# A line through HBM in place of a spreading product for four norms, with moved edges and block order

## The chip, the cores and the metric

The kernel runs on one core of one Trainium2 chip. The core has TensorE (PE in the profile; PEld is its weight load), VectorE (DVE), ScalarE (ACT), GpSimd (POOL) and SyncE (SP, which here mostly issues DMA transfers). SBUF is the on-chip memory with 128 partitions, PSUM the memory into which TensorE accumulates. The metric is the device time of the program in microseconds, as the median of several runs. Times inside the program are from one profiled execution, counted from the start of its span.

## The reference

A two-layer decoder trunk over 512 tokens of width 1024, in float32. Cut to its steps:

```python
def rmsnorm(x, g):
    return x * lax.rsqrt(jnp.mean(x * x, axis=-1, keepdims=True) + EPS) * g

h = x
# layer 0
h = h + mixer_a(rmsnorm(h, norm_mix[0]))     # gelu(xn @ w_in) -> u, v; u * (W_s norm(v) + b) @ w_out
h = h + conv_ffn(rmsnorm(h, norm_ffn[0]))    # width-3 causal conv between up (1024 -> 2 x 2816) and silu(g)*u, then down
h = h + (p[0] @ w_pin) * sigmoid(rmsnorm(h, norm_ple[0]) @ w_gate + b_gate)
k, v = shared_kv(h, norm_kv, w_kv)
# layer 1
h = h + mixer_b(rmsnorm(h, norm_mix[1]), k, v)   # 16 query heads on 4 KV heads, window of 128, ALiBi, sinks
h = h + conv_ffn(rmsnorm(h, norm_ffn[1]))
h = h + (p[1] @ w_pin) * sigmoid(rmsnorm(h, norm_ple[1]) @ w_gate + b_gate)
return rmsnorm(h, norm_final)
```

Each rmsnorm needs one root per token. The norms are called n0 (norm_mix 0), nf0 (norm_ffn 0), np0 (norm_ple 0), n1 (norm_mix 1 and the shared K/V's gain), nf1 and np1 in the kernel.

## The kernel before, in words

**Layout.** The residual `h` lies transposed: eight tiles of 128 features x 512 tokens. A product of a weight and an activation is made of three float32r products (`mm3`, L190 to L192): high part times high, high times low, low times high. Each is one matmul of 128x128 weights on 512 columns. `mm3t` (L201 to L203) does the same with tokens on the output's partitions.

**Weights.** They arrive on SyncE's queue in pieces (`load`, L136) into a few raw buffers, and are cut in units of up to 1024 columns (`pump`): ScalarE casts the high part `wh` (L163) and VectorE subtracts to get the low part `wl` (L164). There are four unit buffers. `chunk` takes the next units and pumps up to `ahead` units further. The order in which a program line calls `pump` and `chunk` is the order in which casts and differences stand on ScalarE and VectorE; a raw buffer is free for the next load when its last difference has been made.

**Norms.** The gain is multiplied into the activations when they are split, and the root is applied after the product, since it is the same for all features of a token. `Norm.take` splits a tile and adds up its square; `turn` transposes the sum and reduces it (`quarter`, L313). `begin` makes a small product `ms` (L322) with the matrix `alike`, a scale and offset on VectorE (L364) and the power -1/2 on GpSimd (L366), giving `r`: the roots of 512 tokens as 8 columns, token 64*c + p on partition p, twice. Then it casts `r` to a high and a low half (`hl`). `rstd` (L353 to L356) calls `spread`: VectorE multiplies `hl` with a picked identity into `d` (128x512, L346), TensorE multiplies `d` with a matrix of ones (L350), so that every partition holds the whole line of 512 roots, and ScalarE copies it from PSUM to SBUF (L355). The readers multiply a product in PSUM by that line: `uz` (L594) for n0, `hs` (L403) for nf0 and nf1, `z` (L479) for np0. In `ffn` and `ple` `begin` is called after the first product of the block and `rstd` after the second; the readers come right after it. In n0 `begin` is called within the v products and `rstd` before the u products.

**Attention.** Sixteen steps work on score blocks. The dictionary `beside` (L763) gives what TensorE does between the steps: the products of the output projection w_o (`merge`), whose weights come in four chunks c = 0 to 3, and `more`, which pumps one unit ahead. `behind` adds an ordering edge between two instructions of one engine.

**The end.** The last per-layer embedding is computed with tokens on partitions. Block i (128 tokens) is computed in stretches n of 512 or fewer columns: `gate_t` makes its product `gt`, `gated_t` (L999) the sigmoid (`st`), the product with `pet` (L1016), the sum `hm` (L1032), its squares and the gain (L1044, L1048); `scaled` takes the root, `leaves` scales and sends the block. Block 3 has the stretches (3,0), (3,1), (3,2) and is sent by `end` in three pieces.

At the start of the program eight `idle` products (L240) run on TensorE before the first real one.

Of the kernel before, what the change touches and what calls it, by code (L numbers as in the profile page):

```python
# [8 lines left out]
F32 = mybir.dt.float32  # L9
F32R = mybir.dt.float32r  # L10
AF = mybir.ActivationFunctionType
# [32 lines left out]
FIRST = [(0, 0, 1), (1, 0, 1), (0, 1, 2), (1, 1, 2), (0, 2, 4), (0, 4, 8), (1, 2, 4), (1, 4, 8)]  # L44
IDLE = 8


@with_exitstack
def tile_yoco(ctx: ExitStack, tc: tile.TileContext, t, out: bass.AP, out_b: bass.AP):
# [7 lines left out]
    mp = ctx.enter_context(tc.tile_pool(name="mp", bufs=1))  # L57
    tp = ctx.enter_context(tc.tile_pool(name="tp", bufs=2))
    mmp = ctx.enter_context(tc.tile_pool(name="mmp", bufs=8, space=bass.MemoryType.PSUM))

# [218 lines left out]
    class Norm:  # L279


        def __init__(self, name, gains):
            self.name = name
            self.xs = [(xtiles(pool, f"{name}{i}", tags), g) for i, (pool, tags, g) in enumerate(gains)]
            self.acc = self.quarter = self.behind = None

# [28 lines left out]

        def begin(self, rows=1):


            if self.quarter is None:
                self.turn()  # L320
            ps = psum(f"{self.name}ms")[:, : S // 32]
            nc.tensor.matmul(ps, alike.rearrange("p a b -> p (a b)"), self.quarter, start=True, stop=True)  # L322
            ms = ps.rearrange("p (c r) -> p r c", r=2)
            n = S // 64
            r = inv_root([(slice(32 * q, 32 * (q + 1)), ms[32 * q : 32 * (q + 1), q % 2, :]) for q in range(4)],
                         self.name, n=n)
            def by_rows():
                self.rt = const.tile([P, NC], F32, tag="rows", bufs=2, name=f"{self.name}rows")
                r2 = r.rearrange("p (c e) -> p e c", e=2)
                for e in range(2):  # L330
                    nc.vector.tensor_copy(self.rt[64 * e : 64 * (e + 1)], r2[64 * e : 64 * (e + 1), e])

            if rows == 1:
                by_rows()

            self.hl = const.tile([P, n], F32R, tag="hl", bufs=1, name=f"{self.name}hl")
            nc.vector.tensor_copy(self.hl, r)
            nc.vector.tensor_sub(self.hl[64:], r[64:], self.hl[64:].bitcast(F32))
            if rows == 2:
                by_rows()  # L340
            return self.rt if rows else None
# [10 lines left out]

        def rstd(self):  # L353
            r = tp.tile([P, S], F32, tag="rstd", name=f"{self.name}rstd")
            nc.scalar.copy(r, self.spread(0, S // 64))  # L355
            return r  # L356
# [30 lines left out]
    def ffn(l, norm, nxt):  # L387
# [4 lines left out]
        def up(j):  # L392
            parts = chunk(256, KD)
            pss, cs = [], []
            for s in range(2):
                ps = psum(f"up{j}_{s}")
                mm3(ps, parts, xs, s * P)
                pss.append(ps)
                if j == 0:
                    rstds.append(norm.rstd() if s else norm.begin(rows=0))  # L400
            for s, ps in enumerate(pss):
# [63 lines left out]
    def ple(l, norm, nxt, pe):  # L465
        xs = norm.xs[0][0]
        rstd, held = None, []
        for c in range(4):
            parts = chunk(256, KD)
            for j in range(2):  # L470
                ps = psum(f"gate{c}_{j}")
                mm3(ps, parts, xs, j * P)
                held.append((2 * c + j, ps))
                if c == 0:
                    rstd = norm.rstd() if j else norm.begin(rows=0)
                if c or j:
                    for m, ps in held:
                        z = tp.tile([P, S], F32, tag="hs", name=f"z{m}")
                        nc.vector.tensor_mul(z, ps, rstd)  # L479
                        sg = tp.tile([P, S], F32, tag="sg", name=f"gs{m}")  # L480
                        nc.scalar.activation(sg, z, AF.Sigmoid, bias=v("ple_b_gate", l * KD + m))
                        nc.vector.tensor_mul(sg, sg, pe[m])
                        nc.vector.tensor_add(h[m], h[m], sg)
                        nxt.take(m)
                    held = []
# [15 lines left out]
    for q, k0, k1 in FIRST:  # L501
# [28 lines left out]
        if (q, k0) == (1, 2):  # L530
            rt = n0.begin()
    vps[0][0] = zv[0][:, :S]
# [80 lines left out]

    dram = ctx.enter_context(tc.tile_pool(name="dram", bufs=1, space=bass.MemoryType.DRAM))
    lines = dram.tile([KD, 2, P], F32, name="lines")
# [49 lines left out]
    def queries(ps, g, j):  # L665
# [15 lines left out]
        nc.scalar.copy(hi.bitcast(F32R), qf)  # L681
        nc.vector.tensor_sub(qf.bitcast(F32R), qf, hi)
        for e, q in enumerate(res):
# [62 lines left out]
    def merge(m, k0, k1, leave=False):  # L746


        if m // 2 not in box:
            box[m // 2] = chunk(256, KD, ahead=2)  # L750
        first = k0 == 0 or box.get(f"left{m}", False)
        if first:
            box[f"o{m}"] = psum(f"o{m}_{k0}")
        mm3(box[f"o{m}"], box[m // 2][k0:k1], o2[k0:k1], m % 2 * P, first=first, last=leave or k1 == KD)
        box[f"k{m}"], box[f"left{m}"] = k1, leave
        if leave:
            nc.vector.tensor_add(h[m], h[m], box[f"o{m}"])

    def more():

        pump(state["unit"] + 1)

    beside = {  # L763
# [13 lines left out]
        12: [(merge, 1, 2, 4, True), (merge, 2, 2, 4)],  # L777
        13: [(merge, 3, 0, 4), (more,)],
        14: [(merge, 4, 0, 4)],
        15: [(merge, 5, 0, 4)],  # L780
        16: [(merge, 2, 4, 6), (merge, 3, 4, 6), (merge, 0, 4, 6), (merge, 1, 4, 6)],
# [14 lines left out]
    def scores(i):  # L796
# [8 lines left out]
        for b in range(2):  # L805
# [8 lines left out]
            for j in range(2):  # L814
                e = 2 * b + j
                hd = GQ * g + e
                nc.vector.tensor_tensor_reduce(out=pr[:, e, :P], in0=far if n else near, in1=sc[:, j, 0, :],
                                               scale=-slope(hd), scalar=nsink[:, hd : hd + 1],
                                               op0=ALU.add, op1=ALU.min, accum_out=neg[:, e : e + 1])
        sm = at.tile([P, GQ], F32, tag="sm", bufs=2, name=f"sm{i}")  # L820
        for e in range(GQ):
            nc.scalar.activation(pr[:, e, :], pr[:, e, :], AF.Exp, bias=neg[:, e : e + 1], scale=-1.0,
                                 accum_out=sm[:, e : e + 1])
        live[i] = (pr, sm)
# [37 lines left out]
    def mix(i):  # L862
# [15 lines left out]
        for e in range(2):  # L878
            nc.vector.tensor_add(o[sides[e]], a[:, e], low[:, e])
        cols = slice(n * P, (n + 1) * P)  # L880
# [120 lines left out]
    def gated_t(i, n, ps):  # L1001
# [4 lines left out]
        if end:  # L1006
            box["sg"] = nc.scalar.activation(sg, ps, AF.Sigmoid, scale=r)
        else:
# [34 lines left out]
        if i < LAST:  # L1043
            nc.gpsimd.tensor_mul(hm, hm, grow[:, c0 : c0 + w])  # L1044
        else:
# [12 lines left out]
    def leaves(i, root):  # L1058
# [3 lines left out]
        for n in range(2):  # L1062
# [7 lines left out]
            if i == 2:  # L1070
                behind(ins, box["sg"])
            if i == 0:
# [13 lines left out]
    def end():  # L1086
        y = yt[0]
        nc.gpsimd.tensor_tensor(rfin, total[:, 2:3], minus_half[:, :1], op=ALU.pow)
        for c0, c1 in ((0, 384), (384, 640), (640, D)):
            if c0:  # L1090
# [12 lines left out]
    bias_rows()  # L1103
    for i, n in ((2, 0), (3, 0), (2, 1)):
        gated_t(i, n, gate_t(i, n))
    root = scaled(2)
    for n in (1, 2):
        gated_t(3, n, gate_t(3, n))
    leaves(2, root)
    end()  # L1110


# [64 lines left out]
```

## Time and profile before

| | |
|---|---|
| median of 3 runs | 1131.25 us (1131.01 to 1131.46) |
| the profiled execution's own time | 1131.34 us |
| its span | 1129.6 us |
| mean granted TensorE clock | 0.998 |
| busy: PE, DVE, ACT, POOL | 1119.6, 760.5, 513.3, 102.9 us |
| DMA | 117.50 MB, mean 104 GB/s |

A row of the timeline has the start, the duration, the engine, the line, the operation with its tiles (output <- inputs), and in brackets how long the engine was idle before it and what ended the idle time. In a row with a count (x2) neighbouring instructions are put together. The duration of a matmul is 0.39 us, but the matmuls overlap; one starts every 0.22 us. The chain that ended last is followed back from the program's last instruction, with its start, length, engine and line. The DMA rows have the destination, the source, the queue, the count, the KB of each and the median us from issue to landing.

### The profile page before, as it was taken

How to read it: one execution, taken by the hardware profiler on the slowest of the kernel's cores; microseconds unless marked ns; L12 is line 12 of the kernel's file. 1: busy time of each engine (PE TensorE's matmuls, PEld its weight loads, DVE VectorE, ACT ScalarE, POOL GpSimd, SP SyncE). 2: the span in 40 equal slices, each digit the busy share in tenths (PEclk: the TensorE clock that was granted, in tenths of full speed). 3: DMA queues.
4: the chain of work that ended last, by engine and by line, in shares of the span. 5: the costliest groups of instructions: out<-in, count | busy, mean ns of one | idle time of the engine just before them, and what ended most of it. 6: DMA issues, size and time to landing. Idle time of an engine off the chain costs nothing.

```text
span 1129.6 us, 13299 instructions
## 1 busy us (share of the span) xinstructions
PE 1119.6 (99%) x5117; PEld 930.5 (82%) x5117; DVE 760.5 (67%) x1174; ACT 513.3 (45%) x811; POOL 102.9 (9%) x163
## 2 busy tenths in 40 slices
PE   9999999999999999999999999999999999999997
PEld 7888888888888888888888888888888888888886
DVE  5566477763577457656988997777636773675686
ACT  5733344441344234544656775444313432344543
POOL 1100210000000000022204441000000000000211
PEclk9999999999999999999999999999999999999999
DMA  8322323223132222323134223323232233224333
GB/s 305 130 96 75 112 75 112 88 99 112 75 103 83 100 106 89 102 108 112 53 97 131 75 94 115 133 89 112 77 110 100 78 103 112 83 80 154 107 97 78
DMA packets 35424, 117.50 MB, mean 104 GB/s; under 512 B 11672, under 2 KB 17568, under 8 KB 25888
## 3 DMA queue, kind: packets, MB, share of 16 engines
q1 hardware_dynamic: 34944, 116.19, 30.8%
q8 instruction: 40, 0.66, 0.2%
q10 hardware_dynamic: 416, 0.46, 0.1%
q14 instruction: 24, 0.20, 0.1%
HBM read 108.24 MB, written 2.11 MB: 98 GB/s over the span
## 4 chain that ended last, share of the span: by engine, by line
PE 93%; DVE 4%; ACT 1%; issue 1%; DMA 0%; POOL 0%; POOLq 0%; SPq 0%; DVEq 0%; ACTq 0%
PE up L190 14%; PE up L192 14%; PE up L191 14%; PE d L192 8%; PE d L190 8%; PE d L191 8%; PE gate L190 1%; PE u L191 1%; PE gate L192 1%; PE u L190 1%; PE u L192 1%; PE gate L191 1%; PE gt L201 1%; PE v L201 1%; PE gt L203 1%; PE v L203 1%
## 5 line engine op out<-in xcount | busy, mean ns | idle before, releaser
L164 DVE TENSOR_TENSOR wl<-wraw,wh 128x1024 fp32r<-128x1024 f32 (+1 forms) x198 | 238.2, 1205 | 123.9 <-ACT wh L163 123.5
L163 ACT CAST wh<-wraw 128x1024 fp32r<-128x1024 f32 (+2 forms) x197 | 201.9, 1028 | 261.5 <-PE d L191 131.6
L190 PE MATMUL up<-nf00h,wh 128*128 128x512 f32 x352 | 137.1, 390 | 0.0
L190 PE MATMUL up<-nf10h,wh 128*128 128x512 f32 x352 | 137.0, 389 | 0.0
L192 PE MATMUL up<-nf00h,wl 128*128 128x512 f32 x352 | 137.0, 389 | 0.0
L192 PE MATMUL up<-nf10h,wl 128*128 128x512 f32 x352 | 137.0, 389 | 0.0
L191 PE MATMUL up<-nf10l,wh 128*128 128x512 f32 x352 | 137.0, 389 | 0.0
L191 PE MATMUL up<-nf00l,wh 128*128 128x512 f32 x352 | 137.0, 389 | 0.0
L190 PE MATMUL d<-ah,wh 128*128 128x512 f32 x352 | 136.9, 389 | 0.0
L191 PE MATMUL d<-al,wh 128*128 128x512 f32 x352 | 136.9, 389 | 0.0
L192 PE MATMUL d<-ah,wl 128*128 128x512 f32 x352 | 136.9, 389 | 0.0
L407 ACT ACTIVATE c<-hs,vec 128x512 f32<-128x512 f32 x88 | 71.5, 815 | 72.8 <-DVE hs L403 72.1
L408 DVE SCALAR_TENSOR_TENSOR c<-hs,vec,c 128x511 f32<-128x511 f32 x88 | 65.8, 748 | 34.2 <-ACT c L407 34.2
L383 DVE TENSOR_TENSOR h<-h,d 128x512 f32<-128x512 f32 x56 | 38.4, 686 | 73.0 <-PE d L192 73.0
L191 PEld LDWEIGHTS up<-nf00l,wh 128*128 128x128 f32 x352 | 66.1, 188 | 13.8
L192 PEld LDWEIGHTS up<-nf10h,wl 128*128 128x128 f32 x352 | 66.1, 188 | 13.8
L191 PEld LDWEIGHTS d<-al,wh 128*128 128x128 f32 x352 | 66.1, 188 | 13.7
L190 PEld LDWEIGHTS up<-nf10h,wh 128*128 128x128 f32 x352 | 66.1, 188 | 13.7
L192 PEld LDWEIGHTS d<-ah,wl 128*128 128x128 f32 x352 | 66.1, 188 | 13.7
L190 PEld LDWEIGHTS d<-ah,wh 128*128 128x128 f32 x352 | 66.1, 188 | 13.7
L192 PEld LDWEIGHTS up<-nf00h,wl 128*128 128x128 f32 x352 | 66.1, 188 | 13.7
L190 PEld LDWEIGHTS up<-nf00h,wh 128*128 128x128 f32 x352 | 66.1, 188 | 13.6
(406 smaller groups left out, 1953.3 us busy)
## 6 DMA issues: line engine op xcount, KB each, us to landing
wraw<-in_w_up SPq DMA_DIRECT2D x44, 1024.0 KB, 4.7
wraw<-in_w_down SPq DMA_DIRECT2D x16, 896.0 KB, 4.6
wraw<-in_w_down SPq DMA_DIRECT2D x8, 1024.0 KB, 5.0
wraw<-in_w_gate SPq DMA_DIRECT2D x8, 1024.0 KB, 4.8
wraw<-in_w_u SPq DMA_DIRECT2D x4, 1024.0 KB, 6.9
wraw<-in_w_out SPq DMA_DIRECT2D x4, 1024.0 KB, 4.8
wraw<-in_w_q SPq DMA_DIRECT2D x4, 1024.0 KB, 5.1
wraw<-in_w_o SPq DMA_DIRECT2D x4, 1024.0 KB, 4.9
```

What stands on the lines that cost most here:

```text
L163: cast = nc.scalar.copy(hi, src)
L164: state["split"] = cast, nc.vector.tensor_sub(low, src, hi.bitcast(F32))
L190: nc.tensor.matmul(ps, wh[:, a:b], xh, start=st, stop=False)
L191: nc.tensor.matmul(ps, wh[:, a:b], xl, start=False, stop=False)
L192: nc.tensor.matmul(ps, wl[:, a:b], xh, start=False, stop=en)
L201: nc.tensor.matmul(ps, xh[:, s], wh[:, a:b], start=st, stop=False)
L203: nc.tensor.matmul(ps, xh[:, s], wl[:, a:b], start=False, stop=en)
L383: nc.vector.tensor_add(h[m], h[m], ps)
L407: nc.scalar.activation(c, hs, AF.Identity, bias=v("conv_b", l * 2 * NJ + col), scale=cw[2])
L408: nc.vector.scalar_tensor_tensor(c[:, 1:], hs[:, : S - 1], cw[1], c[:, 1:], op0=ALU.mult, op1=ALU.add)
```

## The change

- Four norms, n0, nf0, np0 and nf1, are begun with `line=True` and `halves=False`. Right after the power GpSimd's DMA queue writes the 512 roots from 64 partitions into a line in HBM, and `rstd` reads this line back on the same queue, broadcast to all 128 partitions. Their casts into halves, the product `d`, the product with ones and the copy fall away. n1 and np1 keep the spread.
- The number of idle products is 9 in place of 8.
- At the end of attention, the difference that makes the low part of the last queries (`box["low", 3, 1]`) stands behind the sum of step 7 (`i == 7`). The third chunk of w_o is taken in two halves, and its second half is pumped in step 15 (`more` with 15) in place of step 13, with the cast behind the last exponential of that step and the difference behind its last maximum.
- At the end of the program, the gain of block 2 is multiplied by VectorE in place of GpSimd; the order of blocks is (2,0), (2,1), (3,0), sending block 2, (3,1), (3,2), in place of (2,0), (3,0), (2,1), (3,1), (3,2), sending block 2; block 2's scaling stands behind the sigmoid of (3,0) in place of the last one; the pieces of block 3 are 384, 384 and 256 columns in place of 384, 256 and 384.

```diff
-IDLE = 8
+IDLE = 9
...
+    dram = ctx.enter_context(tc.tile_pool(name="dram", bufs=1, space=bass.MemoryType.DRAM))
...
-        def begin(self, rows=1):
+        def begin(self, rows=1, halves=True, line=False):
...
             if rows == 1:
                 by_rows()
+            if line:
+                self.line = dram.tile([S], F32, name=f"{self.name}line")
+                nc.gpsimd.dma_start(self.line.rearrange("(c p) -> p c", p=64), r[:64])
+            if not halves:
+                return self.rt if rows else None
...
         def rstd(self):
+
             r = tp.tile([P, S], F32, tag="rstd", name=f"{self.name}rstd")
-            nc.scalar.copy(r, self.spread(0, S // 64))
+            if self.line is not None:
+                nc.gpsimd.dma_start(r, self.line.partition_broadcast(P))
+            else:
+                nc.scalar.copy(r, self.spread(0, S // 64))
             return r
...
-                    rstds.append(norm.rstd() if s else norm.begin(rows=0))
+                    rstds.append(norm.rstd() if s else norm.begin(rows=0, halves=False, line=True))
...
-                    rstd = norm.rstd() if j else norm.begin(rows=0)
+                    rstd = norm.rstd() if j else norm.begin(rows=0, halves=False, line=True)
...
-            rt = n0.begin()
+            rt = n0.begin(halves=False, line=True)
...
-        nc.vector.tensor_sub(qf.bitcast(F32R), qf, hi)
+        box["low", g, j] = nc.vector.tensor_sub(qf.bitcast(F32R), qf, hi)
...
-        if m // 2 not in box:
-            box[m // 2] = chunk(256, KD, ahead=2)
+        c = m // 2
+        if c not in box:
+            box[c] = chunk(256, KD // 2, ahead=1) if c == 2 else chunk(256, KD, ahead=2)
+        if len(box[c]) < k1:
+            box[c] += chunk(256, KD // 2, ahead=1)
...
-    def more():
+    def more(step=None):
         pump(state["unit"] + 1)
+        if step is not None:
+            for ins, front in zip(state["split"], box["done", step]):
+                behind(ins, front)
...
-        13: [(merge, 3, 0, 4), (more,)],
+        13: [(merge, 3, 0, 4)],
         14: [(merge, 4, 0, 4)],
-        15: [(merge, 5, 0, 4)],
+        15: [(merge, 5, 0, 4), (more, 15)],
...
+        if i == 7:
+            behind(box["low", 3, 1], ins)
...
         if i < LAST:
-            nc.gpsimd.tensor_mul(hm, hm, grow[:, c0 : c0 + w])
+            nc.vector.tensor_mul(hm, hm, grow[:, c0 : c0 + w])
...
             if i == 2:
-                behind(ins, box["sg"])
+                behind(ins, box["sg", 3, 0])
...
-        for c0, c1 in ((0, 384), (384, 640), (640, D)):
+        for c0, c1 in ((0, 384), (384, 768), (768, D)):
...
-    for i, n in ((2, 0), (3, 0), (2, 1)):
-        gated_t(i, n, gate_t(i, n))
+    for n in range(2):
+        gated_t(2, n, gate_t(2, n))
     root = scaled(2)
+    gated_t(3, 0, gate_t(3, 0))
+    leaves(2, root)
     for n in (1, 2):
         gated_t(3, n, gate_t(3, n))
-    leaves(2, root)
     end()
```

More of the change, by code (lines that the diff above doesn't have):

```diff
@@ L284, in __init__ @@
             self.xs = [(xtiles(pool, f"{name}{i}", tags), g) for i, (pool, tags, g) in enumerate(gains)]
-            self.acc = self.quarter = self.behind = None
+            self.acc = self.quarter = self.behind = self.line = None
         def split(self, k, i):
@@ L611, in tile_yoco @@
     dense_add(us, KD, nf)
-    dram = ctx.enter_context(tc.tile_pool(name="dram", bufs=1, space=bass.MemoryType.DRAM))
     lines = dram.tile([KD, 2, P], F32, name="lines")
@@ L753, in merge @@
             box[f"o{m}"] = psum(f"o{m}_{k0}")
-        mm3(box[f"o{m}"], box[m // 2][k0:k1], o2[k0:k1], m % 2 * P, first=first, last=leave or k1 == KD)
+        mm3(box[f"o{m}"], box[c][k0:k1], o2[k0:k1], m % 2 * P, first=first, last=leave or k1 == KD)
         box[f"k{m}"], box[f"left{m}"] = k1, leave
@@ L816, in scores @@
                 hd = GQ * g + e
-                nc.vector.tensor_tensor_reduce(out=pr[:, e, :P], in0=far if n else near, in1=sc[:, j, 0, :],
+                most = nc.vector.tensor_tensor_reduce(out=pr[:, e, :P], in0=far if n else near, in1=sc[:, j, 0, :],
                                                scale=-slope(hd), scalar=nsink[:, hd : hd + 1],
@@ L821, in scores @@
         for e in range(GQ):
-            nc.scalar.activation(pr[:, e, :], pr[:, e, :], AF.Exp, bias=neg[:, e : e + 1], scale=-1.0,
-                                 accum_out=sm[:, e : e + 1])
+            ins = nc.scalar.activation(pr[:, e, :], pr[:, e, :], AF.Exp, bias=neg[:, e : e + 1], scale=-1.0,
+                                       accum_out=sm[:, e : e + 1])
+        box["done", i] = ins, most
         live[i] = (pr, sm)
@@ L878, in mix @@
         for e in range(2):
-            nc.vector.tensor_add(o[sides[e]], a[:, e], low[:, e])
+            ins = nc.vector.tensor_add(o[sides[e]], a[:, e], low[:, e])
+        if i == 7:
+            behind(box["low", 3, 1], ins)
         cols = slice(n * P, (n + 1) * P)
@@ L1006, in gated_t @@
         if end:
-            box["sg"] = nc.scalar.activation(sg, ps, AF.Sigmoid, scale=r)
+            nc.scalar.activation(sg, ps, AF.Sigmoid, scale=r)
         else:
```

## The prediction

> **What bounds the kernel now.** I read the page first (busy shares and the chain that ended last), then TensorE's waits and start times, then the stretch around each of the four norms, then the end.
>
> ```profile
> PE 1119.6 (99%) x5117; PEld 930.5 (82%) x5117; DVE 760.5 (67%) x1174; ACT 513.3 (45%) x811; POOL 102.9 (9%) x163
> PE 93%; DVE 4%; ACT 1%; issue 1%; DMA 0%; POOL 0%; POOLq 0%; SPq 0%; DVEq 0%; ACTq 0%
> ```
>
> TensorE (PE) is busy for 99% of the span and carries 93% of the chain that sets the end; VectorE (DVE) has a third of its time free, GpSimd (POOL) nine tenths. So a change pays where it takes work out of PE's stream, where it closes one of PE's few gaps, or behind the last matmul. It costs where another engine, idle on average, is late for PE at one place. The profiled execution took 1131.34 us (span 1129.6 and 1.74 around it), 0.09 over the median of 1131.25; the sum below is made on 1131.34.
>
> **The change part by part.**
>
> *Four spreads less on PE.* Each norm of the four loses one 128x512 product:
>
> ```profile
> 49.85 0.24 PE n0sp L350
> ...
> 717.56 0.24 PE nf1sp L350
> ```
>
> The first and last of four such rows in the chain, about 0.235 each: 4 x 0.235 = -0.94 us. They stand on the chain, so the gain is full as long as nothing takes their place. The copy out of PSUM that goes with each (0.58 of ScalarE, ACT, in the 527.22 row below) and the small products on DVE lie beside PE and count for nothing, except where DVE is the tight engine (np0, below).
>
> *A ninth idle product.*
>
> ```profile
> 1.12 3.78 PE L240 MATMUL idle<-idle 128*128 128x512 f32 x8 [1.12 <-DVE minus_half L243]
> 5.29 1.02 PE L511 MATMUL v<-wh,n00h 128*128 128x512 f32 x2 [0.39 <-ACT n00h L264]
> ```
>
> The eight idle products end at 4.90, 3.78/8 = 0.47 each, and the first real one waits for ACT until 5.29. A ninth ends at about 5.37 and fills this gap: 0, and +-0.3 for the range.
>
> *Attention's end.* The queries' low part and the cut of w_o's third chunk are moved so that DVE reaches the two things PE waits for sooner:
>
> ```profile
> 652.71 0.41 PE L190 MATMUL o<-oh,wh 128*128 128x512 f32 x1
> 653.35 0.50 PE L191 MATMUL o<-ol,wh 128*128 128x512 f32 x1 [0.23 <-POOL ol L884]
> 666.47 1.23 DVE L164 TENSOR_TENSOR wl<-wraw,wh 128x1024 fp32r<-128x1024 f32 x1
> 667.72 0.33 SPq L136 DMA_DIRECT2D wraw<-in_w_o  x1
> 670.48 0.36 PE L810 MATMUL sc<-kh,q 128*128 128x256 f32 x1 [0.18 <-DVE neg L817]
> 684.68 0.50 ACT L883 CAST oh<-side 128x128 fp32r<-128x128 f32 x2 [0.91 <-DVE side L879]
> ```
>
> Elsewhere PE issues one such product in 0.22 (15.00 us for 68, window rows below), so from 652.71 to 653.35 PE loses 0.41, and about 0.2 more beside it: 0.6. At 670.48 it loses 0.34 behind the maxima (neg) of step 15. If both go, -0.95. But w_o's last chunk goes through one raw buffer, and its load (667.72) is released by the difference at 666.47. That difference now stands behind step 15's maxima and exponentials, near 678 (an estimate: the maxima end at 670.48, and exponentials and reduction follow), so the load of 1 MB starts ten us later and lands, by the row below, near 683; ACT's cast of it is in the program ahead of the `oh` cast at 684.68, and DVE's difference ahead of step 15's sum. I let that give back 0.45 of the 0.95: -0.5, with ends -0.95 and +0.5.
>
> ```profile
> wraw<-in_w_o SPq DMA_DIRECT2D x4, 1024.0 KB, 4.9
> ```
>
> *The tail.* One multiplication goes from POOL to DVE, block (2,1) goes ahead of (3,0), the last output piece becomes 256 columns instead of 384.
>
> ```profile
> 1119.49 1.29 POOL L1044 TENSOR_TENSOR hm<-hm,row_m 128x512 f32<-128x512 f32 x1 [5.18 <-ACT sqt L1034]
> 1120.09 0.97 DVE L1016 TENSOR_TENSOR st<-st,pet 128x256 f32<-128x256 f32 x1 [0.23 <-issue]
> 1121.58 0.47 ACT L1007 ACTIVATE st<-gt,np1rows 128x256 f32<-128x256 f32 x1 [1.86 <-PE gt L203]
> 1121.97 0.42 DVE L1048 TENSOR_TENSOR yt<-hm,row_m 128x256 f32<-128x256 f32 x1
> 1122.31 0.42 DVE L1016 TENSOR_TENSOR st<-st,pet 128x256 f32<-128x256 f32 x1
> out<-yt SPq DMA_DIRECT2D x1, 192.0 KB, 3.0
> out<-yt SPq DMA_DIRECT2D x1, 128.0 KB, 1.7
> ```
>
> While POOL multiplies, the DVE product at 1120.09 takes 0.97 against 0.42 for the same form at 1122.31: 0.55 lost on DVE, which carries over in part to the `yt` at 1121.97, and this one holds the 1122.31 product 0.3 past ACT's end at 1122.05. The DVE gets the 512-wide product instead (two of the 256 form, 0.8), but earlier, while PE still has (3,1) and (3,2) to run. The end is a 128 KB landing in place of 192 KB, or the reverse, since the rows give 1.7 for 128 KB and 3.0 for the 192 KB issued just ahead. I take -0.4, ends -0.8 and +0.1.
>
> *The round trip, R.* A root is now written to HBM by POOL's queue and read back, 256 KB to all partitions; R is the time from the end of `pow` to the line in SBUF. POOL's own queue carries no transfer in this trace, and so R is bounded by SyncE's:
>
> ```profile
> vec<-in_vec SPq DMA_DIRECT2D x1, 4.0 KB, 2.7
> out<-hm SPq DMA_DIRECT2D x2, 256.0 KB, 2.1
> row_m<-lines SPq DMA_DIRECT2D x2, 512.0 KB, 4.5
> sink<-in_sinks SPq DMA_DIRECT2D x1, 8.0 KB, 11.0
> ```
>
> Low end: two landings of 1.7 to 2.1 and one issue of 0.33, 4.1. High end: two of 4.5 and two issues of 1, 11 (the sinks' 11.0 for 8 KB is a queue's backlog and shows that a small transfer can be that late). Nearest rows: 2.7 for the write, whose 2 KB is nearest to the 4 KB of `vec`; for the read halfway between 2.1 (its bytes) and 4.5 (a spread over partitions like its own), 3.3; and half a us for the second issue: R = 6.5.
> The Trainium skill, "DMA: Bandwidth & Descriptors", section "Anatomy of one DMA — SWDGE (gpsimd) path", puts one such transfer at 2.0 us and its bytes at 436 GB/s; by this the two together would be an estimated 4.6 us, inside these ends, and no run here shows it yet. The same page, "Rules for kernel authors", says that an access whose last dimension isn't contiguous becomes a descriptor for each element, which speaks against the change: the write is 512 elements of 4 bytes.
>
> Who waits for R, norm by norm:
>
> ```profile
> 39.79 1.67 POOL L366 TENSOR_TENSOR n0rt<-n0m,minus_half 128x8 f32<-128x8 f32 x1 [10.02 <-DVE n0m L364]
> 58.51 0.69 DVE L594 TENSOR_TENSOR uz<-u,n0rstd 128x512 f32<-128x512 f32 x1
> ...
> 150.97 1.65 POOL L366 TENSOR_TENSOR nf0rt<-nf0m,minus_half 128x8 f32<-128x8 f32 x1 [8.59 <-DVE nf0m L364]
> 157.90 1.29 DVE L403 TENSOR_TENSOR hs<-up,nf0rstd 128x512 f32<-128x512 f32 x2
> 169.69 0.39 PE L191 MATMUL up<-nf00l,wh 128*128 128x512 f32 x1
> ```
>
> n0: the first reader is 58.51 - 41.46 = 17 us behind the root: nothing. nf0: `hs` started 157.90 - 152.62 = 5.28 behind. A later line moves it, and the wl difference (1.23) that the change puts behind it on DVE; with R = 11 the two `hs` and this wl end near 152.62 + 11 + 1.29 + 1.23 = 166.1, and PE wants that wl about 169.6: nothing up to R = 14. nf1 is the same loop in layer 1: nothing.
>
> np0 is the tight one:
>
> ```profile
> 521.68 1.65 POOL L366 TENSOR_TENSOR np0rt<-np0m,minus_half 128x8 f32<-128x8 f32 x1 [7.69 <-DVE np0m L364]
> 527.22 0.58 ACT L355 COPY np0rstd<-np0sp 128x512 f32<-128x512 f32 x1
> 527.35 1.23 DVE L164 TENSOR_TENSOR wl<-wraw,wh 128x1024 fp32r<-128x1024 f32 x1 [1.49 <-ACT wh L163]
> 528.61 1.29 DVE L479 TENSOR_TENSOR z<-gate,np0rstd 128x512 f32<-128x512 f32 x2
> 534.49 1.34 POOL L298 TENSOR_TENSOR n1acc<-n1sq,n1sq 128x512 f32<-128x512 f32 x1 [11.16 <-ACT n1sq L293]
> 565.85 0.74 DVE L265 SCALAR_TENSOR_TENSOR n10l<-h,vec,n10h 128x512 fp32r<-128x512 f32 x1
> 568.28 0.39 PE L191 MATMUL k<-n10l,wh 128*128 128x512 f32 x1
> 569.04 0.67 DVE L313 TENSOR_REDUCE n1quarter<-n1turn 128x16 f32<-128x512 f32 x1
> 570.09 0.29 PE L322 MATMUL n1ms<-n1quarter,alike 128*128 128x16 f32 x2
> ```
>
> ```profile
> 530.00:545.00 15.00, 15.00 (x68) 12.43 (x67) 13.91 (x17) 8.94 (x15) 2.80 (x3) 1.00 0.17 67
> 560.00:570.00 10.00, 10.00 (x46) 8.29 (x45) 10.00 (x15) 6.25 (x10) 0.99 (x1) 1.00 0.30 107
> ```
>
> The root is there at 523.33, `z0` starts 5.28 later. In between DVE did wl (1.23), which the new order puts behind `z0` and `z1`. The two window rows (the window, its length, then the busy time of PE, weight load, DVE, ACT and POOL with counts) show DVE 13.91 of 15 and 10.00 of 10 us busy: with its backlog never drained, a `z0` that starts late moves everything to the end of the block, 30 us on. There `n10l` ends at 566.59 with 1.7 in hand before PE wants it, but n1quarter ends at 569.71 and PE takes it at 570.09: 0.4 in hand, 0.15 once PE has run ahead by its own saved spread. So PE waits R - 5.3, less the at most 0.9 that DVE's small gaps and that slack can take, plus what wl behind `z` costs: about R - 5.3 when R is above it. At R = 6.5: +1.2. What is queued on POOL behind the second transfer, which waits for the first to land, is n1's sum of squares at 534.49, 11 us after the root; it is led by the late `z` anyway.
>
> *Sum:* -0.94 + 0 - 0.5 - 0.4 + 1.2 = -0.64, so 1130.7 on the profiled time and 1130.6 on the median.
>
> **The rivals.**
>
> *A: the trip is hidden at np0 too (R up to 5.3).* For: the low end of 4.1, and 2.1 for 256 KB in the output's row. Against: the two transfers are in series, and 4.5 is the only row of a broadcast. Sum -1.84, 1129.4; with both other parts at their best ends, and the ninth product worth its 0.3, -0.94 - 0.95 - 0.8 - 0.3 = -2.99, 1128.3.
> By the Trainium skill's formula quoted above this is the case (4.6 is under 5.3), and the sum would then be the 1129.4 worked out here; as the traces stand, with no transfer on that queue, I give it 3 in 10.
>
> *B, the other side: the write of 512 scattered elements, or the read behind weight loads on the same 16 DMA engines, makes R at np0 long.* At R = 11 PE stands still for 5.7 before n1's products: -1.84 + 5.7 = +3.9, 1135.1; at R = 9.4 the sum is +2.26, the point from which the kernel counts as slower. For: the sinks' row at 11.0, the 1 MB weight loads of 4.6 to 5 us that run all the time. Against: every other small row is under 5 us.
>
> *C: the third chunk of w_o is later than I allow.* ACT's cast and DVE's difference of it then hold `oh` and step 15's sum, and PE's merge of the last heads: +1.5 in place of -0.5, with the rest as forecast, +1.36, 1132.6. For: the load starts ten us later. Against: PE has other merges (step 14, 15) to run meanwhile.
>
> *D: nothing happens.* PE's saved products turn into waits for the same DVE and DMA ends (PE's slack to n1quarter is 0.4, less than three spreads), and the tail hangs on the same last landing: 1131.2.
>
> **How the numbers follow.** About 0.2% (2.26 us, so 1128.99 and 1133.51) is what a measurement of this kernel tells from no change. Chances: my forecast (R from 5.3 to 8, 1129.0 to 1132.6 with the ends of the other parts) 0.40, A 0.30, B 0.15, C 0.08, D 0.07. Faster by over 0.2% needs A with most of its best ends, or a trip as in A and a tail worth more than I see: 0.27. Slower: B from R = 9.4, and C or the forecast with several high ends: 0.22. Within: 0.51. The likeliest one's own range is 1129.0 to 1132.6; for 8 in 10, with A's best end and B up to R of about 9.8, 1128.2 to 1133.9.
>
> **What the new profile would show.** The spread rows of the four norms gone and PE's pitch unbroken there; on POOL two transfers behind each `pow`, their landings apart by R. `z0` at 523.3 + R less what PE gained, and a wait of PE on n1quarter near 570, equal to R - 5.3: that row decides between forecast, A and B. At 652 and 670 the two gaps gone; a new wait of PE near 684 on `oh` would be C. In the tail the 1120.09 row at 0.42 and the last matmul nearer to the end of the span. Wrong would be: a PE wait at nf0 or nf1 (R over 14), a DVE slowed by POOL's descriptor writing, or a head in which the first real product starts later than 5.4.

## The result and the profile after

The changed kernel takes 1138.95 us (median of 6 runs, 1138.06 to 1139.62), the kernel before 1131.09 us (6 runs): a ratio of 1.007, interval 1.0059 to 1.0081. It is slower by 7.9 us, where 0.6 us faster was forecast. The profiled execution took 1139.62 us with a span of 1137.9, 8.3 over the one before, and its runs scatter more than those of the kernel before.

The page of the changed kernel (engine busy times and the chain's shares), then its TensorE waits: engine, line, what it waited for, total, times, longest.

```profile
span 1137.9 us, 13283 instructions
PE 1122.5 (99%) x5114; PEld 932.3 (82%) x5114; DVE 751.7 (66%) x1164; ACT 511.8 (45%) x807; POOL 107.7 (9%) x169
PE 94%; DVE 3%; DMA 1%; issue 1%; ACT 0%; POOL 0%; POOLq 0%; DVEq 0%
```

```profile
PE k L191 <- ACT n10h L265: 5.0, 2, 4.8
PE idle L241 <- DVE minus_half L244: 1.1, 1, 1.1
PE k L192 <- DVE n10l L266: 1.0, 3, 0.4
PE sc L825 <- PE sc L826: 0.3, 1, 0.3
```

A new wait of 4.8 us stands first, on `n10h`, at the products of K; the two waits at attention's end (`ol`, `neg`) are gone, and one of 0.3 on `sc` has come there. PE's busy time grew although four products of work are gone: some of its products took longer, as shown below.

Where the time went can be read from the start of the same product in the two traces. The shift, after minus before:

| product | before | after | shift | step |
|---|---|---|---|---|
| first gate product after np0's spread | 526.53 | 525.74 | -0.79 | three spreads gone |
| n1's mean of squares (`n1ms`) | 570.09 | 578.71 | +8.62 | +9.4 |
| third product after it (`q`) | 570.77 | 579.99 | +9.22 | +0.6 |
| first product after nf1's mean of squares | 711.85 | 720.61 | +8.76 | -0.46, attention's end |
| first product after nf1's spread | 717.64 | 726.16 | +8.52 | -0.24, the fourth spread |
| end of the last product | 1121.54 | 1130.02 | +8.48 | 0 |
| end of the span | 1129.6 | 1137.9 | +8.3 | -0.2, tail |

All of the loss lies between np0's roots and the first products behind `n1ms`, some 55 us on. There the rows of GpSimd and VectorE (timeline: start, duration, engine, line, operation; in brackets the idle time before it and what ended it) read:

```profile
521.13 1.67 POOL L376 TENSOR_TENSOR np0rt<-np0m,minus_half 128x8 f32<-128x8 f32 x1 [7.69 <-DVE np0m L374]
523.09 0.77 POOL L338 DMA_DIRECT2D np0line<-np0rt  x1 [0.29 <-POOL np0rt L376]
532.72 0.59 POOL L363 DMA_DIRECT2D np0rstd<-np0line  x1 [8.85 <-DMA np0line<-np0rt]
...
536.97 1.29 DVE L489 TENSOR_TENSOR z<-gate,np0rstd 128x512 f32<-128x512 f32 x2 [11.67 <-DMA np0rstd<-np0line]
...
574.34 0.74 DVE L266 SCALAR_TENSOR_TENSOR n10l<-h,vec,n10h 128x512 fp32r<-128x512 f32 x1
577.52 0.68 DVE L314 TENSOR_REDUCE n1quarter<-n1turn 128x16 f32<-128x512 f32 x1
```

The root is there at 522.80, `z` starts at 536.97: the round trip took R = 14.17 us, of which GpSimd sat 8.85 behind the write. `z` starts 8.36 later than before, the last `n10l` 8.49 and `n1quarter` 8.48: VectorE carried the delay through to its last instruction of the block without giving any of it back.

The transfers of the four norms, with the median us from issue to landing:

```profile
np0line<-np0rt POOLq DMA_DIRECT2D x1, 2.0 KB, 9.1
nf0line<-nf0rt POOLq DMA_DIRECT2D x1, 2.0 KB, 9.4
n0line<-n0rt POOLq DMA_DIRECT2D x1, 2.0 KB, 9.9
nf1line<-nf1rt POOLq DMA_DIRECT2D x1, 2.0 KB, 8.6
np0rstd<-np0line POOLq DMA_DIRECT2D x1, 256.0 KB, 4.2
n0rstd<-n0line POOLq DMA_DIRECT2D x1, 256.0 KB, 6.3
```

The write of 2 KB takes longer than the read of 256 KB at all four places: 2.2 times as long at np0, 1.6 times at n0.

Then TensorE's own rows behind the wait, and the windows around it (window, its length, busy time of PE, weight load, DVE, ACT, POOL with counts, granted clock, DMA share, GB/s):

```profile
568.73 0.40 PE L193 MATMUL k<-n10h,wl 128*128 128x512 f32 x1
573.90 0.79 PE L191 MATMUL k<-n10h,wh 128*128 128x512 f32 x1 [4.78 <-ACT n10h L265]
...
576.15 0.63 PE L191 MATMUL k<-n10h,wh 128*128 128x512 f32 x1
576.58 0.63 PE L192 MATMUL k<-n10l,wh 128*128 128x512 f32 x1
```

```profile
560.00:568.00 8.00, 7.45 (x31) 5.33 (x29) 7.18 (x11) 6.19 (x10) 1.34 (x2) 1.00 0.35 133
568.00:574.00 6.00, 0.90 (x4) 0.40 (x3) 6.00 (x9) 4.70 (x8) 1.48 (x1) 0.94 0.42 132
574.00:580.00 6.00, 5.56 (x14) 4.12 (x15) 5.89 (x12) 3.07 (x4) 0.00 (x0) 0.50 0.10 42
580.00:585.00 5.00, 5.00 (x23) 4.17 (x22) 2.38 (x7) 0.00 (x0) 1.66 (x1) 0.99 0.00 2
```

After the standstill the granted clock is 0.50 for some six microseconds, and products start every 0.43 instead of 0.23. That is a second cost, which the prediction's steps did not have.

### The profile page after: what moved, and what is told of

It reads as the page before. It is cut to its first block, busy times and chain, and to the rows that moved or that the text cites. A ratio compares the mean times of both kernels' runs of the same rounds, so it can differ in the third digit from the quotient of the medians.

```text
span 1137.9 us, 13283 instructions
## 1 busy us (share of the span) xinstructions
PE 1122.5 (99%) x5114; PEld 932.3 (82%) x5114; DVE 751.7 (66%) x1164; ACT 511.8 (45%) x807; POOL 107.7 (9%) x169
## 4 chain that ended last, share of the span: by engine, by line
PE 94%; DVE 3%; DMA 1%; issue 1%; ACT 0%; POOL 0%; POOLq 0%; DVEq 0%
PE up L193 14%; PE up L191 14%; PE up L192 14%; PE d L193 8%; PE d L191 8%; PE d L192 8%; PE q L191 1%; PE q L192 1%; PE o L192 1%; PE o L191 1%; PE q L193 1%; PE o L193 1%; PE u L192 1%; PE u L191 1%; PE u L193 1%; PE pv L887 1%
## 5 line engine op out<-in xcount | busy, mean ns | idle before, releaser
L192 PEld LDWEIGHTS up<-nf10l,wh 128*128 128x128 f32 x352 | 66.1, 188 | 13.8
L192 PEld LDWEIGHTS d<-al,wh 128*128 128x128 f32 x352 | 66.1, 188 | 13.8
L193 PEld LDWEIGHTS up<-nf00h,wl 128*128 128x128 f32 x352 | 66.1, 188 | 13.8
```

The source lines that it names most:

```text
L192: nc.tensor.matmul(ps, wh[:, a:b], xl, start=False, stop=False)
L193: nc.tensor.matmul(ps, wl[:, a:b], xh, start=False, stop=en)
```

## The experiments

Three questions: is np0's trip all of the loss, why does a write of 2 KB take 9 us, and what are the other parts worth? Times of the kernel before, in the groups of runs that each experiment was measured with, were 1130.88 to 1131.07. Where two kernels differ by half a microsecond, medians and traces are read together.

### np0 alone

One norm back on the spread:

```diff
-                    rstd = norm.rstd() if j else norm.begin(rows=0, halves=False, line=True)
+                    rstd = norm.rstd() if j else norm.begin(rows=0)
```

> The changed kernel with one norm, np0, put back on the spreading product; n0, nf0 and nf1 keep the line through HBM, all other parts stay. Theory 'the trip at np0 alone': VectorE gets the roots of np0 late by the trip, everything that it feeds up to n1 is late with it, and nothing else costs; then this is faster than the kernel before by three spreads (0.7 us), 0.3 to 0.5 at attention's end and 0.2 in the tail: 1129.6 to 1130.1 us. Rival 'the other trips or the moved edges cost too': it stays above 1131.5.

Measured: 1129.46 us (11 runs, 1129.0 to 1129.98) against 1130.94, ratio 0.9986, interval 0.9977 to 0.9996. That is a little faster than the theory's range. With one of the four norms taken out of the change, the change is worth 1.5 us. Its TensorE waits have no row of np0 or n1 left:

```profile
PE idle L241 <- DVE minus_half L244: 1.1, 1, 1.1
PE sc L825 <- PE sc L826: 0.3, 1, 0.3
```

The counterpart, the kernel before with np0 alone on the line:

```diff
-                    rstd = norm.rstd() if j else norm.begin(rows=0)
+                    rstd = norm.rstd() if j else norm.begin(rows=0, halves=False, line=True)
```

> The kernel before with one edit: np0 goes through HBM. Theory 'the trip at np0 alone': about 9.5 us slower than before (the ten us that the trace of the changed kernel loses between np0 and n1, less one spread and what TensorE isn't ahead here): 1140 to 1141. Rival 'it needs the other edits': less than half of this, under 1136.

Measured: 1139.82 us, ratio 1.0077 (1.0063 to 1.0091), 8.9 slower than before: a little less than expected (in its profile the write landed in 8.1 us and not 9.1), and far over the rival's bound. Both runs together settle that np0's trip is the loss; at the other three trips no wait of TensorE shows.

### Why the write takes 9 us

The same 2 KB in 64 pieces of 32 bytes, in place of 512 of 4 bytes:

```diff
-                nc.gpsimd.dma_start(self.line.rearrange("(c p) -> p c", p=64), r[:64])
+                nc.gpsimd.dma_start(self.line.rearrange("(p c) -> p c", p=64), r[:64])
```

> The changed kernel, but each partition writes its 8 roots as one piece of 32 bytes in place of 8 pieces of 4 bytes (64 pieces in place of 512, the same 2 KB). Tokens get the root of another token, all else is the same work. Theory 'pieces': the write's landing of 9.1 us is the 512 pieces of 4 bytes; it falls to 2 to 4, z0 comes 5 to 7 us sooner and the kernel takes 1130.5 to 1133. Rival 'queue': a transfer on this queue takes 9 us to be seen whatever its shape; the time stays within 1 us of 1139.

Measured: 1130.48 us (10 runs, 1129.8 to 1130.79), ratio 0.9995 (0.9986 to 1.0004). Its DMA rows and its `z`:

```profile
np0line<-np0rt POOLq DMA_DIRECT2D x1, 2.0 KB, 1.7
np0rstd<-np0line POOLq DMA_DIRECT2D x1, 256.0 KB, 3.6
```

```profile
520.99 1.67 POOL L376 TENSOR_TENSOR np0rt<-np0m,minus_half 128x8 f32<-128x8 f32 x1 [7.69 <-DVE np0m L374]
...
528.80 1.29 DVE L489 TENSOR_TENSOR z<-gate,np0rstd 128x512 f32<-128x512 f32 x2 [3.64 <-DMA np0rstd<-np0line]
```

The write falls from 9.1 to 1.7 and R from 14.17 to 528.80 - 522.66 = 6.14; `z` comes 8.2 sooner, more than the expected 5 to 7. The write's form was the cause, not the way through HBM.

The same 512 pieces, issued by SyncE:

```diff
-                nc.gpsimd.dma_start(self.line.rearrange("(c p) -> p c", p=64), r[:64])
+                nc.sync.dma_start(self.line.rearrange("(c p) -> p c", p=64), r[:64])
```

> The changed kernel, with the write of the line issued by SyncE in place of GpSimd, still in 512 pieces of 4 bytes; the read stays on GpSimd. Theory 'pieces': the landing stays at 8 to 10 us and the time at 1137 to 1140. Rival 'queue': the landing falls to 2 to 3 us, the rows of SyncE for small transfers, and the kernel takes 1130 to 1133.

Measured: 1138.13 us (1137.21 to 1139.29), ratio 1.0064 (1.005 to 1.0078).

```profile
nf0line<-nf0rt SPq DMA_DIRECT2D x1, 2.0 KB, 8.8
nf1line<-nf1rt SPq DMA_DIRECT2D x1, 2.0 KB, 8.6
```

The profile gives no landing for np0's own write, but GpSimd waits 10.32 for it before it can issue the read:

```profile
532.49 0.60 POOL L363 DMA_DIRECT2D np0rstd<-np0line  x1 [10.32 <-DMA np0line<-np0rt]
```

The landing is as long on another queue: GpSimd's queue is not the cause.

At this point 'pieces of 4 bytes' looked settled. The next run put np0's 512 pieces far apart:

```diff
+    apart = dram.tile([128 * S], F32, name="apart")
+    nc.gpsimd.dma_start(apart[:S].rearrange("(p c) -> p c", p=64), ident[:64, :8])
...
+                if self.name == "np0":
+                    nc.gpsimd.dma_start(apart.rearrange("(p c o) -> p c o", p=64, o=128)[:, :, 0], r[:64])
+                    self.line = apart[:S]
```

> The changed kernel; np0 alone writes its 512 pieces of 4 bytes 512 bytes apart from each other, and reads back 2 KB of the same buffer (so np0's roots are not the right ones; the work is the same, with one small write at the start). Theory 'number': each piece of 4 bytes costs, wherever it goes; the landing stays at 8 to 10 us, the time at 1138 to 1140. Rival 'shared lines': pieces of neighbouring partitions wait for each other since they lie within the same few bytes of HBM; apart, the landing falls to 2 to 4 us and the time to 1130.5 to 1132.5.

Measured: 1130.85 us (10 runs, 1130.63 to 1131.32), ratio 1.0 (0.9991 to 1.0009); its write, the first of the rows below, landed in 2.2. The theory 'number' fell: 512 pieces of 4 bytes cost only 0.5 us more than 64 of 32 bytes, when they lie apart. How far apart, and apart from whom, was left to three runs in which only the order and the distance `o` differ: 8 bytes (`o=2`) with each partition's eight pieces in 64 bytes of their own; 64 bytes (`o=16`); and 8 bytes in the order of the tokens (`"(c p o) -> p c o"`), where the eight pieces in 64 bytes come from eight partitions.

> As the kernel whose pieces lie 512 bytes apart (write landed in 2.2 us, 1130.85), but the 512 pieces of np0 lie 8 bytes apart, each partition's eight in a block of 64 bytes of its own; np0's roots are again not the right ones. Theory 'shared between partitions': it is enough that no two partitions write into the same 64 bytes; landing 2 to 3 us, 1130.4 to 1131.3. Rival 'any two pieces within a few bytes': eight small writes into one block hold each other up as well; landing 4 us or more, 1132 or more.

> The same with the 512 pieces 64 bytes apart, neighbours of different partitions and of the same one alike in blocks of their own. Theory 'a block of 64 bytes': landing 2 to 3 us and 1130.4 to 1131.3, as at 512 bytes. Rival 'a larger block': landing stays over 4 us, 1132 or more.

> As the kernel with pieces 8 bytes apart (eight of one partition in a block of 64 bytes: landing 3.7 us, 1132.5), but in the order of the tokens: the eight pieces of a block come from eight partitions. np0's roots are again not the right ones. Theory 'shared between partitions': the same count in a block costs more when it comes from several partitions; landing 5 us or more, 1134 or more. Rival 'count in a block': the same as there, landing 3.2 to 4.2 us, 1132 to 1133.

Measured: 1132.49, 1131.08 and 1132.59 us, ratios 1.0012 (1.0003 to 1.0022), 1.0001 (0.9992 to 1.0011) and 1.0014 (1.0004 to 1.0024). The row of np0's write in each, one fence for each kernel: 512 bytes apart, 64 bytes, 8 bytes with one partition in a block, 8 bytes with eight.

```profile
apart<-np0rt POOLq DMA_DIRECT2D x1, 2.0 KB, 2.2
```

```profile
apart<-np0rt POOLq DMA_DIRECT2D x1, 2.0 KB, 2.2
```

```profile
apart<-np0rt POOLq DMA_DIRECT2D x1, 2.0 KB, 3.7
```

```profile
apart<-np0rt POOLq DMA_DIRECT2D x1, 2.0 KB, 3.9
```

So what counts is how densely the small writes lie in HBM: with one in 64 bytes 2.2 us, with eight 3.7 to 3.9, with sixteen (the line of the change) 9.1. In the same four kernels the lines of n0, nf0 and nf1, left as the change has them, took 7.5 to 9.6. That the writes come from different partitions matters little (3.7 against 3.9), so my theory 'shared between partitions' fell as well. With eight partitions in a block its rival held; with one, its rival held by the time (1132.49) and missed by the landing (3.7, not 4 or more). The runs change the distance between neighbours (4, 8, 64 bytes) and the number in a block of 64 bytes together, so whether the block or the distance counts, and whether 64 bytes is the size that matters, isn't shown. The steps are not even, 1.6 us for the first seven neighbours and 5.3 for the next eight; why is left open.

### A right line in larger pieces

If np0's transposition deals the tokens out in blocks of eight, each partition holds eight neighbouring roots, and its 32 bytes are one piece of the right line:

```diff
-            nc.vector.transpose(sq, self.acc)
+            if self.name == "np0":
+                nc.vector.transpose(sq.rearrange("p (r c i) -> p r c i", r=2, c=8),
+                                    self.acc.rearrange("p (r i c) -> p r c i", r=2, c=8))
+            else:
+                nc.vector.transpose(sq, self.acc)
...
-            ms = ps.rearrange("p (c r) -> p r c", r=2)
+            ms = ps.rearrange("p (r c) -> p r c" if self.name == "np0" else "p (c r) -> p r c", r=2)
...
+                if self.name == "np0":
+                    nc.gpsimd.dma_start(self.line.rearrange("(p c) -> p c", p=64), r[:64])
...
```

> The changed kernel, with np0's tokens put in another order by the transposition (blocks of 8 neighbouring tokens for each partition), so that each partition writes one piece of 32 bytes and the line is right. Theory 'pieces': like the kernel whose partitions all wrote one piece, z0 about 6 us after the root and 1130.2 to 1130.9; the kernel is between the one with np0 on the spread and the one before. Rival 'the transposition pays': VectorE reads the sum of squares with a stride and takes longer for it than the 0.7 us, and the time is above 1131.5.

Measured: 1130.60 us (11 runs, 1130.14 to 1131.4), ratio 0.9997 (0.9988 to 1.0007). The strided transposition costs 0.45 us more (1.16 against 0.71), the write lands in 1.7:

```profile
518.25 1.16 DVE L313 STREAM_TRANSPOSE np0turn<-np0acc 128x512 f32<-128x512 f32 x1
```

This gets all but 1.1 us of the loss against the kernel with np0 on the spread back. About half of that is R itself: `n1ms` still waits 0.56 for `n1quarter`. The rest isn't assigned.

```profile
PE n1ms L327 <- DVE n1quarter L318: 0.6, 1, 0.6
```

### The clock

20 products without use in the place of the standstill:

```diff
...
+    mm3(kps[0], parts[6:7], xkv[6:7], 0, first=False, last=False)
+    fill = psum("fill").rearrange("p (a b) -> p a b", a=4)
+    for i in range(FILL):
+        nc.tensor.matmul(fill, ones, ones.rearrange("p (o t) -> p o t", o=1).to_broadcast([P, 4, P]),
+                         start=True, stop=True)
+    mm3(kps[0], parts[7:], xkv[7:], 0, first=False)
...
```

> The changed kernel with 20 products without use on TensorE (4.5 us at full clock) at the place where it stands still for the last n10h before n1. Theory 'clock': after that wait the records show a granted clock of 0.5 for some six us; with TensorE busy the clock stays at 1.0, and since half of the slow products lie beside the wait for n1quarter anyway, 0.7 to 1.3 us are gained: 1137.6 to 1138.3. Rival 'only the wait': what follows the standstill is late by its data alone; no gain (within 0.4 of 1139) or a loss, as the 20 products run past the data's arrival.

Measured: 1137.14 us (4 runs, 1136.7 to 1137.9), 1.8 less than the changed kernel and under the theory's range. Its windows over the same stretch:

```profile
568.00:574.00 6.00, 5.38 (x23) 3.88 (x21) 6.00 (x9) 4.70 (x8) 0.70 (x1) 1.00 0.50 175
574.00:580.00 6.00, 4.64 (x20) 3.60 (x21) 5.11 (x11) 2.31 (x3) 0.77 (x1) 1.00 0.01 1
```

The clock stays at 1.00. Not all of the gain is the clock. The profiled executions differ by 1.7 us; in this one np0's write happened to land sooner, and `z` started at 536.18 instead of 536.97, 0.79 of it. What is left is 0.9, and the rows agree: `n1ms` comes 0.06 behind the end of `n1quarter` instead of 0.51, and up to the third product behind it TensorE loses 0.11 instead of 0.60 against the kernel before, together 0.9. The Trainium skill, "TensorE: Matmul & The Clock Gate", Part 1, says that the clock falls to half when TensorE stands idle for a window of about 3.4 us; the wait of 4.78 followed by a granted clock of 0.50 agrees.

### The other parts

On the kernel with np0 on the spread (1129.46), first the tail as before:

```diff
...
-            nc.vector.tensor_mul(hm, hm, grow[:, c0 : c0 + w])
+            nc.gpsimd.tensor_mul(hm, hm, grow[:, c0 : c0 + w])
...
-                behind(ins, box["sg", 3, 0])
+                behind(ins, box["sg"])
...
-        for c0, c1 in ((0, 384), (384, 768), (768, D)):
+        for c0, c1 in ((0, 384), (384, 640), (640, D)):
...
-    for n in range(2):
-        gated_t(2, n, gate_t(2, n))
+    for i, n in ((2, 0), (3, 0), (2, 1)):
+        gated_t(i, n, gate_t(i, n))
     root = scaled(2)
-    gated_t(3, 0, gate_t(3, 0))
-    leaves(2, root)
     for n in (1, 2):
         gated_t(3, n, gate_t(3, n))
+    leaves(2, root)
```

> The kernel with np0 on the spread (1129.5), with the tail as before: gain on GpSimd, the old order of blocks, the old cuts. Theory 'small tail': 0.1 to 0.4 us slower than that kernel, 1129.6 to 1129.9, as the traces show 0.17 between the last product and the end. Rival 'my -0.4 and more': slower by over 0.6, above 1130.1.

Measured: 1130.14 us (11 runs, 1129.53 to 1130.52), 0.68 more by the medians, which is just inside the rival's range and outside the theory's. In the profiled executions the time from the end of the last product to the end of the span is 8.31 against 7.88, which is 0.43. The rest, 0.29, is there already at `n1ms` (569.85 against 569.56), ahead of the tail, where the two kernels are the same, and is scatter of the executions. The kernel before, with the same tail, has 8.06. So the tail is worth 0.2 to 0.4 by the traces and 0.7 by the medians. What it removes is the slow product that the prediction had seen beside GpSimd's multiplication, first with the old tail, then with the new:

```profile
1118.73 1.29 DVE L1034 TENSOR_TENSOR st<-st,pet 128x256 f32<-128x256 f32 x1
```

```profile
1118.43 0.43 DVE L1034 TENSOR_TENSOR st<-st,pet 128x256 f32<-128x256 f32 x1
```

Then attention's end as before:

```diff
...
-            box[c] = chunk(256, KD // 2, ahead=1) if c == 2 else chunk(256, KD, ahead=2)
-        if len(box[c]) < k1:
-            box[c] += chunk(256, KD // 2, ahead=1)
+            box[m // 2] = chunk(256, KD, ahead=2)
...
-        13: [(merge, 3, 0, 4)],
+        13: [(merge, 3, 0, 4), (more,)],
...
-        15: [(merge, 5, 0, 4), (more, 15)],
+        15: [(merge, 5, 0, 4)],
...
-        if i == 7:
-            behind(box["low", 3, 1], ins)
```

> The kernel with np0 on the spread (1129.5), with attention's end as before: w_o's third chunk whole, its cut in step 13, no order for the queries' low part. Theory of the prediction's step: the edits are worth 0.4 to 0.5 us, as the shift of TensorE's rows from 651 to 711 says (-0.40): 1129.8 to 1130.1. Rival: the gaps closed come back elsewhere; within 0.2 of 1129.5.

Measured: 1130.09 us (11 runs, 1129.58 to 1130.54), 0.63 more. The two waits on `ol` and `neg` are back:

```profile
PE o L192 <- POOL ol L897: 0.2, 1, 0.2
PE sc L822 <- DVE neg L829: 0.2, 1, 0.2
```

Between `n1ms` and nf1's mean of squares the traces of the two kernels differ by 0.56 (141.54 against 140.98). Both parts gain about what they were expected to gain; the two differences of medians are small beside the intervals of the three kernels (0.9977 to 0.9996, 0.9984 to 1.0002 and 0.9983 to 1.0001 of the kernel before), which overlap. The best version found is the change without np0's line: 1129.46 us.

## Why the prediction was wrong

**What bounds the kernel** held: PE's stream is the kernel, and one late engine at one place costs what it is late.

**Four spreads, -0.94.** Right: the shifts are about 0.23, 0.28, 0.28 and 0.24.

**The ninth idle product, 0.** Right: the first product starts at 5.13 in place of 5.29, but from 9.98 on the two traces run together.

**Attention's end, -0.5.** Right in size, -0.46 by the two traces and 0.6 by the experiment, but the 0.45 given back in this sum is right by luck. The two gaps closed for 0.64 and 0.34, as predicted. The late load and cast of w_o's third chunk gave nothing back: the shift is +8.77 behind the second gap and +8.76 at nf1, and the wait on `oh` that rival C had near 684 isn't in the new trace (near 693 there). What was lost came between the two gaps, at a score product (655.63 before) that now waits; the kernel with attention's end as before has no such wait:

```profile
662.01 0.39 PE L192 MATMUL o<-ol,wh 128*128 128x512 f32 x1
664.74 0.30 PE L825 MATMUL sc<-kh,q 128*128 128x128 f32 x1 [0.30 <-PE sc L826]
```

The shift is +9.30 ahead of the first gap, +8.66 at the first row (653.35 before) and +9.11 at the second: 0.45 lost. Why this product is held isn't shown.

**The tail, -0.4.** Right within its range: -0.2 by the two traces, 0.4 by the trace and 0.7 by the medians of the experiment, and by the mechanism described.

**n0, nf0, nf1 hidden.** Right, but n0 and nf0 only just. At n0 R was 17.0 against the 17 in hand, and VectorE stood 0.41 for the line at 58.30 without TensorE waiting. To nf0 I had given until R = 14; its R was 13.8 and its late wl is ready at 168.57, where PE wants it about 169.6:

```profile
150.70 1.65 POOL L376 TENSOR_TENSOR nf0rt<-nf0m,minus_half 128x8 f32<-128x8 f32 x1 [8.60 <-DVE nf0m L374]
166.14 1.29 DVE L413 TENSOR_TENSOR hs<-up,nf0rstd 128x512 f32<-128x512 f32 x2 [11.26 <-DMA nf0rstd<-nf0line]
167.35 1.22 DVE L165 TENSOR_TENSOR wl<-wraw,wh 128x1024 fp32r<-128x1024 f32 x1
```

**The round trip, R = 6.5.** This is the step that failed: "2.7 for the write, whose 2 KB is nearest to the 4 KB of `vec`". I chose the nearest row by its bytes, but `vec` is a read, with 32 bytes to a partition; the write of the change is 512 pieces of 4 bytes, sixteen to each 64 bytes of HBM, and landed in 9.1. The read was 4.2 against 3.3. Of the 7.7 by which R was short, the write is 6.4, the read 0.9 and the issues the rest. Nor did the high end hold: 11, from two landings of 4.5 and two issues, against 14.17. I had named the pieces as what spoke against the change and gave them no price of their own. The rule cited for it, that an access without contiguous last dimension becomes a descriptor for each element (the Trainium skill, "DMA: Bandwidth & Descriptors", "Rules for kernel authors"), would not have given it either: the same 512 elements, apart, land in 2.2.
The other rule of the Trainium skill weighed there ("DMA: Bandwidth & Descriptors", "Anatomy of one DMA — SWDGE (gpsimd) path") gives an estimated 2.0 us for the write, where 32-byte pieces took 1.7 and the change's own 9.1, and 2.6 for the read, where the runs show 3.3 to 4.4 at np0.

**np0: PE waits R - 5.3.** Right as a mechanism, and this is rival B. With the measured R the formula gives 14.17 - 5.3 = 8.9, and the whole sum -1.84 + 8.9 = +7.0; measured is +8.3 in the profiled executions and +7.9 by the medians. The difference is the clock, 0.9, and a tail that in this trace gave 0.2 instead of 0.4; 0.2 stay unassigned. With 32-byte pieces R is 6.14, so the formula gives 0.8; the trace shows a wait of 0.8 on `n1quarter`, as the prediction described it. Two more kernels agree: with the right line in larger pieces R is 5.92, the formula gives 0.6 and the wait is 0.56; with 4-byte pieces 512 bytes apart these are 6.36, 1.1 and 1.01. The row of the kernel with 32-byte pieces:

```profile
570.09 0.40 PE L323 MATMUL n1ms<-n1quarter,alike 128*128 128x16 f32 x2 [0.81 <-DVE n1quarter L314]
```

In the changed kernel the wait shows earlier, on `n10h`, since the delay of 8.5 is far more than the 1.7 that `n10l` had in hand.

**The chances.** B had 0.15, with its price worked out only up to R = 11 (+3.9), and the range ended at R = 9.8. The form that a write has in HBM was the unknown cost, and I bounded it by rows none of which had that form.

## What to carry to other kernels

A duration is borrowed from a row of the same form, not of the same size: a write whose pieces are 4 bytes and lie next to each other in HBM took 9 us for 2 KB, and 1.7 when each partition wrote 32 bytes in one piece. A detour through HBM costs nothing where the first reader comes later than the trip, and in full where an engine with a backlog stands behind it: ask it norm by norm, and keep the on-chip way at the one place that is tight (1129.46 against 1138.95). Behind a standstill of TensorE of 4.78 us some six us of half clock cost another 0.9.

## What was not expected of the hardware

- Writes of 4 bytes: 512 of them landed in 2.2 us with one in 64 bytes, in 3.7 to 3.9 us with eight, in 7.5 to 9.9 us with sixteen. These are from GpSimd's queue; on SyncE's the last took 8.6 to 10.0. The same 2 KB in 64 writes of 32 bytes landed in 1.7 to 1.9 us behind the root, and in 2.8 to 3.5 at the start of the program.
- A granted clock of 0.50 for some six us after a wait of 4.78 us, worth 0.9 us here, and none of it when 20 products without use filled the wait.
- The transposition of 128x512 with a strided input took 1.16 us instead of 0.71.
